# Two-head products issued in turn: 64-row tiles in the RWKV layers, 64-column tiles in the SSD layer

## The chip, the cores and the metric

The kernel runs on one core of one Trainium2 chip. TensorE (PE) multiplies; its weight loads are a row of their own in the profile (PEld). VectorE (DVE) and ScalarE (ACT) empty PSUM and do the elementwise work, GpSimd (POOL) and SyncE (SP) mostly issue transfers. The metric is the device time of one execution in microseconds, as the median of the timed runs.

## The reference

A decoder of four layers over 256 tokens of width 2048, batch 1: RWKV-7, gated linear attention (GLA), SSD (Mamba-2) and RWKV-7 again, each behind an RMS norm that is modulated by a condition vector (`ada_w`), each added back through a gate. What matters here is one step of two of the mixers.

RWKV, 32 heads of 64, written as a recurrence over tokens:

```
state = state * w_t - outer(state @ kk_t, kk_t * a_t) + outer(v_t, k_t)
y_t   = state @ r_t
```

The kernel computes it in two chunks of 128 tokens. Per head and chunk it needs products of two 64 x 128 operands over the 64 channels of a head: the 128 x 128 matrix of one operand's tokens against another's.

SSD, 64 heads of 64 in 8 groups, state 128, chunk 128:

```
y_diag = sum_j (C_i . B_j) * decay_ij * x_j      (inside a chunk)
y_off  = C_i @ state_before * exp(acum_i)        (from the chunk before)
y      = y_diag + y_off + d_skip * x
```

For each head that is two 64 x 128 results from the diagonal and one more added to the second.

## The kernel before

All activations are kept as channels on partitions, tokens along the free axis. The four layers run one after the other. A projection (`proj`, `jobs`, `prods`, line 365) streams weight blocks of 512 KB from DRAM, splits each into a high and a low fp32r part (ACT, line 310, then DVE, line 312), and multiplies three of the four cross products: three products of 128 x 128 by 128 x 256 for every 128 rows and 128 columns of weights. Meanwhile the condition's products for the next layers (`ada_group`, lines 275 to 290) are spread over the program. The code is written as a plain sequence; a list scheduler, with its own estimate of when each operand is ready, sets the order of the instructions on each engine. Tiles come from pools with a fixed number of buffers, and a tile waits until the one that had its buffer before is read out. PSUM has eight banks: two for projections (`acc`), one for the condition (`mx`), five for the stage that runs (`banks`).

An RWKV layer has a stage of its own for `rwkv_first` (run for each of eight units of two blocks, four heads, out of the evacuation of the key projection) and one for `rwkv_second` (out of the evacuation of the r projection). Both call `gram`, which is at line 750: for a head's half h (channels 0 to 63 or 64 to 127 of a block) it takes one bank from `b1` and issues four products (line 759) with 64 rows each, so that only the upper or lower half of the array's rows is used. `rwkv_first` calls it for both halves and multiplies each result by norms (line 745) on its way to `unit_inverse`; `rwkv_second` calls it three times for both halves, and a DVE multiplication by a mask empties each bank (lines 798 and 821). In the first stage `b1` has two buffers and `b2` three; in the second `b1` two, `b2` two, `b3` one. Besides `gram`, `b1` serves lines 788, 812, 814 and 882 in the second stage and 692 and 717 in the first; `b2` serves the chain 840, 845, 854 and 855 of the second stage, and the inverse in the first.

In the SSD layer, `ssd_group` runs eight times. For each of four pairs of heads it writes one bank, head u = 0 to partitions 0 to 63 and head u = 1 to 64 to 127 (half of the array's columns each): lines 1338 and 1339 the two diagonal chunks, line 1340 the part from the state, added to 1339's.

A product of plain fp32 operands shows in the trace as two MATMUL records, an fp32r product and a transpose as one.

Of the kernel before, what the change touches and what calls it, by code (L numbers as in the profile page):

```python
# [9 lines left out]
F32 = mybir.dt.float32  # L10
# [5 lines left out]
P = 128  # L16
# [115 lines left out]
class Kern:  # L132
# [55 lines left out]
    def banks(self, ctx, name, **tags):  # L188

        pool = ctx.enter_context(self.tc.tile_pool(name=name, bufs=1, space=bass.MemoryType.PSUM))  # L190

        def giver(tag, n):
            return lambda: pool.tile([P, 512], F32, name=tag, bufs=n)
        return [giver(t, n) for t, n in tags.items()]

# [303 lines left out]
    def _rwkv(self, i, j):  # L499
# [4 lines left out]
        r = self.r  # L504
# [25 lines left out]
        def mix(c):  # L530
            return [mixed(c, k) for k in range(DT)]
# [8 lines left out]
        def keeper(n, each=lambda un: None):  # L540
            def ev(jj, ps):
                t = rk.tile([P, 2, T], F32, name="sp", bufs=4)
                nc.scalar.copy(out=t, in_=ps)
                nc.gpsimd.dma_start(out=spill[n][:, jj:jj + 2, :], in_=t)
                each(jj // 2)
            return ev
# [55 lines left out]

        with ExitStack() as ctx:
            ra = ctx.enter_context(self.tc.tile_pool(name=f"ra{i}", bufs=2))
            self.b1, self.b2 = self.banks(ctx, f"pa{i}", b1=2, b2=3)
            def first(jj, ps):
                keep[jj // 2] = self.rwkv_first(i, j, jj // 2, ps, lora, ra)
            self.proj(win, D, D, mix(1), first)
        with ExitStack() as ctx:
            rb = ctx.enter_context(self.tc.tile_pool(name=f"rb{i}", bufs=2))  # L610
            self.b1, self.b2, self.b3 = self.banks(ctx, f"pb{i}", b1=2, b2=2, b3=1)

            self.St = []
            for n in range(2):
                t = rb.tile([P, 2, 2, 64], F32, name=f"St{n}", bufs=1)
                nc.gpsimd.memset(t, 0.0)
                self.St.append(t)
            units = []

            def second(un):  # L620
                units.append(self.rwkv_second(i, j, un, spill, keep[un], rb, ylast if un == 7 else None))
                next(units[un])
                if un:
                    next(units[un - 1], None)
                next(units[un])
            self.proj(win, 0, D, mix(0), keeper("r", second))
            next(units[-1], None)
# [33 lines left out]
    def rwkv_first(self, i, j, un, kps, lora, ra):  # L661
# [7 lines left out]
        NCH, C, H = 2, 128, 64  # L669
# [5 lines left out]
        def v2(t):  # L675
            return t[:, 0:512].rearrange("p (q t) -> p q t", q=2)
# [7 lines left out]
        kT, tha, S = abk[:, 0, :], abk[:, 1, :], abk[:, 2, :]  # L684
# [4 lines left out]
        for n, (nm, dst, b) in enumerate((("dec", thd, self.hw0), ("iclr", tha, self.ha0))):  # L689
            ps = self.b1()  # L690
            for q in range(2):
                nc.tensor.matmul(ps[:, q * T:(q + 1) * T], w2[0:LORA, n, q * P:(q + 1) * P], lora[nm][0:LORA],  # L692
                                 start=True, stop=True)
# [20 lines left out]
        ps = self.b1()  # L714
# [25 lines left out]
        Lf = ra.tile([P, 8 * C + 16], F32, name="LT", bufs=3)  # L740
        nc.gpsimd.memset(Lf[:, 8 * C:], 0.0)
        LT = Lf[:, 0:8 * C].rearrange("p (m t) -> p m t", t=C)
        for h in range(2):
            g = self.gram(h, [(v2(tha), v2(kT), c, q) for c in range(NCH) for q in range(2)])
            nc.vector.tensor_tensor(out=LT[:, 4 * h:4 * h + 4, :], in0=g,
                                    in1=n2[:, 4 * h:4 * h + 4].unsqueeze(2).broadcast_to([P, 4, C]), op=ALU.mult)
        Tt = self.unit_inverse(LT, Lf, ra)
# [1 line left out]
        nc.sync.dma_start(out=td, in_=Tt)  # L749
        return kd, td  # L750

    def gram(self, h, which):


        C, H = 128, 64
        ps = self.b1()
        r = slice(H * h, H * h + H)
        for n, (s, t, c, q) in enumerate(which):
            self.nc.tensor.matmul(ps[:, n * C:(n + 1) * C], s[r, q, c * C:(c + 1) * C], t[r, q, c * C:(c + 1) * C],  # L759
                                  start=True, stop=True)  # L760
        return ps.rearrange("p (n t) -> p n t", t=C)

    def rwkv_second(self, i, j, un, spill, kept, rb, last):

# [2 lines left out]
        NCH, C, H = 2, 128, 64  # L767
# [5 lines left out]
        Ac, Bc, Kc, Rc = (abkp[:, w] for w in range(4))  # L773
# [12 lines left out]
        ps = self.b1()  # L786
# [4 lines left out]
        def Gt():  # L791
            return rb.tile([P, 4, C], F32, name="G", bufs=7)

        GBR = []
        for h in range(2):
            g = self.gram(h, [(Bc, Rc, c, q) for c in range(NCH) for q in range(2)])
            GBR.append(Gt())
            nc.vector.tensor_tensor(out=GBR[h], in0=g, in1=self.c("kmask", C).unsqueeze(1).broadcast_to([P, 4, C]),
                                    op=ALU.mult)
        def prep(c):  # L800


            tk = rb.tile([P, 3, 2, P], F32, name="tk", bufs=3)
            for w0, ws in ((0, (Bc, Kc)), (2, (vT,))):
                if w0 == 0 and c == NCH - 1:
                    continue
                ps = self.b1()
                for w, src in enumerate(ws):
                    for q in range(2):
                        o, t = ps[:, (2 * w + q) * P:(2 * w + q + 1) * P], src[:, q, c * C:(c + 1) * C]  # L810
                        if w0 == 2:
                            nc.tensor.matmul(o, t, self.c("cen"), start=True, stop=True)
                        else:
                            nc.tensor.transpose(o, t, self.c("ident"))
                n = len(ws)
                nc.scalar.copy(out=tk[:, w0:w0 + n, :, :].rearrange("p w q t -> p (w q t)"), in_=ps[:, 0:n * 2 * P])
            G = []
            for h in range(2):
                g = self.gram(h, [(Kc, t, c, q) for t in (Ac, Rc) for q in range(2)])
                G.append(Gt())  # L820
                nc.vector.tensor_tensor(out=G[h].rearrange("p (w q) t -> p w q t", w=2),  # L821
                                        in0=g.rearrange("p (w q) t -> p w q t", w=2),
                                        in1=self.c("kmask").rearrange("p (w t) -> p w t", w=2).unsqueeze(2)
                                        .broadcast_to([P, 2, 2, C]), op=ALU.mult)
            return tk, G
        first = prep(0)
        yield

        yb = self.b3()
        St = self.St[un % 2]  # L830
        for c in range(NCH):
            tk, G = prep(c) if c else first
            ps = self.b2()
            for q in range(2):
                if c:
                    nc.tensor.matmul(ps[:, q * P:(q + 1) * P], Ac[:, q, c * C:(c + 1) * C], St[:, q].rearrange("p h v -> p (h v)"),
                                     start=True, stop=False)
                for h in range(2):
                    n = 2 * q + h
# [3 lines left out]
            ps = self.b2()  # L843
# [6 lines left out]
            if c < NCH - 1:  # L850
                ps = self.b2()
# [8 lines left out]
            for q in range(2):  # L860
# [3 lines left out]
                for h in range(2):  # L864
                    n = 2 * q + h
# [13 lines left out]
        ps = self.b1()  # L879
# [381 lines left out]
    def ssd_group(self, g, hs, win, acd, tk, due):  # L1261
        nc = self.nc
        sk, su = self.sk, self.su
        C, NH = 128, 64
# [18 lines left out]
        ps = self.b1()  # L1283
# [6 lines left out]
        ps = self.b1()  # L1290
# [26 lines left out]
        for c in range(2):  # L1317
            ps = self.b1()
            for v in range(4):
                nc.tensor.transpose(ps[:, v * P:(v + 1) * P], xT[:, v, c * C:(c + 1) * C], self.c("ident"))  # L1320
            t = su.tile([P, 8, 64], F32, name=f"xc{c}")
# [5 lines left out]
        ps = self.b1()  # L1327
# [4 lines left out]
        yv = su.tile([P, 4, T], F32, name="yv")  # L1332
        for v in range(4):
            ps = self.b1()
            for u in range(2):
                h = 2 * v + u
                r = slice(64 * u, 64 * u + 64)
                nc.tensor.matmul(ps[r, 0:C], xc[0][:, h, :], M[0][:, h, :], start=True, stop=True)
                nc.tensor.matmul(ps[r, C:T], xc[1][:, h, :], M[1][:, h, :], start=True, stop=False)
                nc.tensor.matmul(ps[r, C:T], st[:, h, :], ce[:, h, :], start=False, stop=True)  # L1340
            nc.vector.scalar_tensor_tensor(out=yv[:, v, :], in0=xT[:, v, :], scalar=self.p("ssd_d", 4 * g + v),
                                           in1=ps[:, 0:T], op0=ALU.mult, op1=ALU.add)
# [18 lines left out]
        ps = self.b1()  # L1361
        for c in range(2):
            nc.tensor.matmul(ps[:, c:c + 1], ss[:, c * P:(c + 1) * P], self.c("one", 0, 1), start=True, stop=True)
        r = self.inv_rms(ps, 1.0 / 512, SSM_EPS, self.b1)
# [73 lines left out]
```

## Time and profile before

| | |
|---|---|
| runs | 2950.04, 2953.18, 2945.70 us; median 2950.04 |
| profiled execution | 2968.06 us, span 2966.2 us |
| PE busy | 2840.5 us, 96% (27138 records) |
| DVE, ACT, POOL busy | 2118.3 us (71%), 1396.5 us (47%), 154.3 us (5%) |
| HBM | 226 GB/s over the span |
| mean granted TensorE clock | 0.966 |

The layers lie one after another in the span. The stage of `rwkv_first` runs at about 200 to 520 and 2300 to 2560 us, that of `rwkv_second` at 540 to 870 and 2590 to 2880, SSD from 1400 to 2100. "Busy" of a group of instructions is the time in which at least one of them was under way; since matmuls are pipelined and their records overlap, what a stretch of products costs PE is read from the starts: from the start of its first to the start of what follows it.

### The profile page before, as it was taken

How to read it: one execution, taken by the hardware profiler on the slowest of the kernel's cores; microseconds unless marked ns; L12 is line 12 of the kernel's file. 1: busy time of each engine (PE TensorE's matmuls, PEld its weight loads, DVE VectorE, ACT ScalarE, POOL GpSimd, SP SyncE). 2: the span in 40 equal slices, each digit the busy share in tenths (PEclk: the TensorE clock that was granted, in tenths of full speed). 3: DMA queues.
4: the chain of work that ended last, by engine and by line, in shares of the span. 5: the costliest groups of instructions: out<-in, count | busy, mean ns of one | idle time of the engine just before them, and what ended most of it. 6: DMA issues, size and time to landing. Idle time of an engine off the chain costs nothing.

```text
span 2966.2 us, 66151 instructions
## 1 busy us (share of the span) xinstructions
PE 2840.5 (96%) x27138; PEld 2637.4 (89%) x27138; DVE 2118.3 (71%) x4000; ACT 1396.5 (47%) x2355; POOL 154.3 (5%) x298
## 2 busy tenths in 40 slices
PE   6899999999999999998999999999889999999997
PEld 4788898899997899997999999999779989999997
DVE  5778784666777867777878786887567878565565
ACT  3475564422335544444554454544357566532233
POOL 0010110101100000000000000000001011010100
PEclk8899999999999999999999999999999999999999
DMA  9877777776666777876776666667556666675533
GB/s 341 311 266 244 238 246 248 276 242 219 215 220 209 257 268 264 290 267 213 278 253 214 218 218 219 213 200 219 172 169 222 218 197 203 204 265 159 180 119 113
DMA packets 239135, 673.82 MB, mean 227 GB/s; under 512 B 72272, under 2 KB 78416, under 8 KB 235760
## 3 DMA queue, kind: packets, MB, share of 16 engines
q1 hardware_dynamic: 217904, 580.84, 59.2%
q0 software_dynamic: 20928, 88.75, 8.4%
q8 instruction: 213, 3.49, 0.5%
q14 instruction: 90, 0.74, 0.1%
HBM read 620.66 MB, written 48.82 MB: 226 GB/s over the span
## 4 chain that ended last, share of the span: by engine, by line
PE 77%; DMA 11%; DVE 6%; issue 3%; SPq 2%; ACT 1%; POOL 0%; DVEq 0%; POOLq 0%; ACTq 0%
PE acc L365 57%; DMA raw<-in_ada_w 4%; PE b L759 3%; PE mx L275 2%; DMA raw<-in_rwkv_w_in 2%; PE pv L365 2%; DVE L L312 1%; DVE adaacc L281 1%; DMA sp<-yd 1%; PE b L868 1%; PE b L867 1%; PE b L845 1%; DMA xd<-dx 1%; PE b L692 1%; ACT H L310 1%
## 5 line engine op out<-in xcount | busy, mean ns | idle before, releaser
L365 PE MATMUL acc<-xs,H 128*128 128x256 f32 x8480 | 1635.2, 291 | 17.7 <-DVE xs L381 7.7
L365 PEld LDWEIGHTS acc<-xs,H 128*128 128x128 f32 x8480 | 1349.4, 194 | 64.1 <-issue 23.4
L365 PE MATMUL acc<-xs,L 128*128 128x256 f32 x4240 | 1225.3, 290 | 3.7 <-DVE L L312 3.7
L310 ACT CAST H<-raw 128x1024 fp32r<-128x1024 f32 (+1 forms) x706 | 718.1, 1018 | 1005.2 <-PE acc L365 745.0
L312 DVE TENSOR_TENSOR L<-raw,H 128x1024 fp32r<-128x1024 f32 (+1 forms) x706 | 835.7, 1185 | 370.7 <-ACT H L310 345.3
L365 PEld LDWEIGHTS acc<-xs,L 128*128 128x128 f32 x4240 | 822.3, 194 | 17.4 <-issue 5.8
L281 DVE SCALAR_TENSOR_TENSOR adaacc<-raw,cact,adaacc 128x512 f32<-128x512 f32 x418 | 312.5, 748 | 139.5 <-DMA raw<-in_ada_w 125.9
L365 PE MATMUL acc<-ys,H 128*128 128x256 f32 x1536 | 288.9, 287 | 2.7 <-ACT ys L380 1.9
L365 PEld LDWEIGHTS acc<-ys,H 128*128 128x128 f32 x1536 | 239.9, 191 | 14.0 <-issue 9.5
L365 PE MATMUL acc<-ys,L 128*128 128x256 f32 x768 | 219.4, 286 | 0.0
L365 PEld LDWEIGHTS acc<-ys,L 128*128 128x128 f32 x768 | 146.1, 190 | 4.5 <-issue 4.5
L275 PE MATMUL mx<-raw,cact 128*32 128x128 f32 x2416 | 118.9, 296 | 24.6 <-DMA raw<-in_ada_w 19.9
L403 DVE SCALAR_TENSOR_TENSOR x<-acc,mod,x 128x256 f32<-128x256 f32 x192 | 83.7, 478 | 54.8 <-PE acc L365 54.4
L523 ACT ACTIVATE hn<-x,mod,omu 128x256 f32<-128x256 f32 x192 | 113.2, 599 | 2.7 <-DVE x L514 1.2
L275 PEld LDWEIGHTS mx<-raw,cact 128*32 128x32 f32 x2416 | 65.9, 114 | 52.8 <-DMA raw<-in_ada_w 18.7
L759 PE MATMUL b<-abkp 64*128 64x128 f32 x768 | 105.0, 293 | 0.0
L759 PEld LDWEIGHTS b<-abkp 64*128 64x128 f32 x768 | 88.0, 193 | 13.6 <-issue 4.6
L365 PE MATMUL acc<-H,xs 128*128 128x256 f32 x512 | 97.3, 290 | 0.0
L526 DVE SCALAR_TENSOR_TENSOR xm<-x,par,hn 128x256 f32<-128x256 f32 x192 | 88.7, 479 | 1.5 <-ACT hn L523 0.3
L365 PEld LDWEIGHTS acc<-H,xs 128*128 128x128 f32 x512 | 82.4, 197 | 1.2 <-issue 1.2
L365 PE MATMUL acc<-L,xs 128*128 128x256 f32 x256 | 73.6, 289 | 0.0
L821 DVE TENSOR_TENSOR G<-b,cst 128x512 f32<-128x512 f32 x64 | 43.6, 688 | 35.7 <-PE b L759 35.1
(350 smaller groups left out, 3293.5 us busy)
## 6 DMA issues: line engine op xcount, KB each, us to landing
raw<-in_ada_w SPq DMA_DIRECT2D x384, 512.0 KB, 5.2
raw<-in_rwkv_w_in SPq DMA_DIRECT2D x256, 512.0 KB, 4.9
raw<-in_ssd_w_in SPq DMA_DIRECT2D x128, 512.0 KB, 4.7
raw<-in_gla_w_in SPq DMA_DIRECT2D x96, 512.0 KB, 4.7
raw<-in_ssd_w_out SPq DMA_DIRECT2D x64, 512.0 KB, 4.5
raw<-in_rwkv_w_out SPq DMA_DIRECT2D x48, 512.0 KB, 4.0
abkp<-kd POOLq DMA_DIRECT2D x16, 1024.0 KB, 6.9
raw<-in_gla_w_out SPq DMA_DIRECT2D x32, 512.0 KB, 5.0
```

The lines of the kernel that those rows point to most:

```text
L275: nc.tensor.matmul(ps[32 * e:32 * e + 32, 0:P], self.cact[:, k:k + 1].broadcast_to([P, 32]), raw[:, u, e * P:(e + 1) * P], start=start, st ...
L281: nc.vector.scalar_tensor_tensor(out=acc, in0=raw[:, u, :], scalar=self.cact[:, k:k + 1], in1=acc, op0=ALU.mult, op1=ALU.add)
L310: nc.scalar.copy(out=hi, in_=raw[:, a:a + n])
L312: nc.vector.tensor_tensor(out=lo, in0=raw[:, a:a + n], in1=hi, op=ALU.subtract)
L365: self.nc.tensor.matmul(ps, lhs, rhs, start=first and part == 0 and w is hi, stop=last and w is lo)
L403: nc.vector.scalar_tensor_tensor(out=self.x[:, t, 1:], in0=ps[:, u, :], scalar=gate[:, t:t + 1], in1=self.x[:, t, 1:], op0=ALU.mult, op1=A ...
L523: nc.scalar.activation(t1, x[:, k, 1:], AF.Identity, scale=self.omu[:, col:col + 1], bias=self.mods[(i, 0)][:, k:k + 1])
L526: done[k] = nc.vector.scalar_tensor_tensor(out=xm, in0=x[:, k, 0:T], scalar=self.p("rwkv_mu", col), in1=t1, op0=ALU.mult, op1=ALU.add)
L692: nc.tensor.matmul(ps[:, q * T:(q + 1) * T], w2[0:LORA, n, q * P:(q + 1) * P], lora[nm][0:LORA], start=True, stop=True)
L759: self.nc.tensor.matmul(ps[:, n * C:(n + 1) * C], s[r, q, c * C:(c + 1) * C], t[r, q, c * C:(c + 1) * C], start=True, stop=True)
L821: nc.vector.tensor_tensor(out=G[h].rearrange("p (w q) t -> p w q t", w=2), in0=g.rearrange("p (w q) t -> p w q t", w=2), in1=self.c("kmask ...
L845: nc.tensor.matmul(ps[:, n * H:(n + 1) * H], Tt[:, 4 * h + 2 * c + q, :], Rh[:, n, :], start=True, stop=True)
```

## The change

`gram` no longer takes one half h, but does both: it takes one tile `g2` of two banks and issues, for each of its four operand pairs, the product of the upper half and then that of the lower half, each half into its own bank. Its callers empty the two banks one after the other as before. The two banks come from the other pools: the first stage now has `b1` 1, `b2` 2 and `g2` one tile of two banks (before `b1` 2, `b2` 3), the second `b1` 1, `b2` 1, `b3` 1 and `g2` one tile (before 2, 2, 1). In SSD the products of the two heads of a pair are issued in turn, kind by kind.

```diff
-            self.b1, self.b2 = self.banks(ctx, f"pa{i}", b1=2, b2=3)
+            self.b1, self.b2, self.g2 = self.banks(ctx, f"pa{i}", b1=1, b2=2, g2=1)
...
-            self.b1, self.b2, self.b3 = self.banks(ctx, f"pb{i}", b1=2, b2=2, b3=1)
+            self.b1, self.b2, self.b3, self.g2 = self.banks(ctx, f"pb{i}", b1=1, b2=1, b3=1, g2=1)
...
-    def gram(self, h, which):
+    def gram(self, which):
         C, H = 128, 64
-        ps = self.b1()
-        r = slice(H * h, H * h + H)
+        both = self.g2()
+        ps = [both[:, h, :] for h in range(2)]
         for n, (s, t, c, q) in enumerate(which):
-            self.nc.tensor.matmul(ps[:, n * C:(n + 1) * C], s[r, q, c * C:(c + 1) * C], t[r, q, c * C:(c + 1) * C],
-                                  start=True, stop=True)
-        return ps.rearrange("p (n t) -> p n t", t=C)
+            for h in range(2):
+                r = slice(H * h, H * h + H)
+                self.nc.tensor.matmul(ps[h][:, n * C:(n + 1) * C], s[r, q, c * C:(c + 1) * C], t[r, q, c * C:(c + 1) * C],
+                                      start=True, stop=True)
+        return [p.rearrange("p (n t) -> p n t", t=C) for p in ps]
...
-            for u in range(2):
-                h = 2 * v + u
-                r = slice(64 * u, 64 * u + 64)
+            hr = [(2 * v + u, slice(64 * u, 64 * u + 64)) for u in range(2)]
+            for h, r in hr:
                 nc.tensor.matmul(ps[r, 0:C], xc[0][:, h, :], M[0][:, h, :], start=True, stop=True)
+            for h, r in hr:
                 nc.tensor.matmul(ps[r, C:T], xc[1][:, h, :], M[1][:, h, :], start=True, stop=False)
+            for h, r in hr:
                 nc.tensor.matmul(ps[r, C:T], st[:, h, :], ce[:, h, :], start=False, stop=True)
```

The lines of the changed kernel stand two to three lower: 365 is 367 there, 759 is 762, 788 is 791, 840 is 841, 845 is 846, 854 and 855 are 855 and 856, 867 and 868 are 868 and 869, 1338 to 1340 are 1339, 1341 and 1343. A name such as `b_6725` is a bank of `b1`, `b2` or `b3` with the number of its tile, `g_6709` one tile of two banks.

PE in the second RWKV stage, the products of one unit's second chunk, before:

```order
L759 MATMUL b_6725<-abkp 128x128 x4
L365 MATMUL acc<-xs,H 128x256
L365 MATMUL acc<-xs,L 128x256
L285 MATMUL mx<-adaacc,cst 32x128
L845 MATMUL b_6694<-Rh,Tt 128x64 x4
L854 MATMUL b_6701<-tk 64x64
L759 MATMUL b_6732<-abkp 128x128 x4
L285 MATMUL mx<-adaacc,cst 32x128 x3
```

The same unit's chunk in the changed kernel:

```order
L841 MATMUL b_6671<-tk,G 128x64 x4
L762 MATMUL g_6709<-abkp 128x128 x6
L883 MATMUL b_6660<-cst,Y 128x128 x4
L868 MATMUL b_6670<-tk,G 128x64
L762 MATMUL g_6709<-abkp 128x128 x2
L367 MATMUL acc<-xs,L 128x256
L846 MATMUL b_6678<-Rh,Tt 128x64 x4
```

The two visits of four products of one half have become one of six and one of two, and in both the halves alternate; the lone product of line 854 has left its place between them.

PE in the first RWKV stage, one unit before (`b_3451` takes the upper half, `b_3457` the lower):

```order
L275 MATMUL mx<-raw,cact 32x128 x5
L759 MATMUL b_3451<-abk 128x128
L759 MATMUL b_3457<-abk 128x128
L759 MATMUL b_3451<-abk 128x128 x3
L759 MATMUL b_3457<-abk 128x128 x3
L275 MATMUL mx<-raw,cact 32x128 x3
```

The same unit in the changed kernel:

```order
L367 MATMUL acc<-xs,L 128x256
L367 MATMUL acc<-xs,H 128x256
L762 MATMUL g_3449<-abk 128x128 x8
L367 MATMUL acc<-xs,H 128x256
L367 MATMUL acc<-xs,L 128x256
```

Before, the scheduler had put the first product of each half side by side and then three of each half in a row; now all eight alternate.

PE in the SSD layer, the products of the first group, before (up to the second of its four pairs in the later piece):

```order
L1339 MATMUL b_17239<-M_16856,xc_17214 64x128
L1338 MATMUL b_17247<-M_16845,xc_17207 64x128
L1339 MATMUL b_17247<-M_16856,xc_17214 64x128
L275 MATMUL mx<-raw,cact 32x128 x8
L1340 MATMUL b_17223<-ce,st 64x128
L1338 MATMUL b_17223<-M_16845,xc_17207 64x128
L1339 MATMUL b_17223<-M_16856,xc_17214 64x128
L1340 MATMUL b_17223<-ce,st 64x128
L1340 MATMUL b_17231<-ce,st 64x128
```

The same group in the changed kernel:

```order
L1339 MATMUL b_17207<-M_16813,xc_17175 64x128 x2
L1341 MATMUL b_17207<-M_16824,xc_17182 64x128 x2
L1339 MATMUL b_17215<-M_16813,xc_17175 64x128 x2
L1341 MATMUL b_17215<-M_16824,xc_17182 64x128 x2
L277 MATMUL mx<-raw,cact 32x128 x2
L1343 MATMUL b_17191<-ce,st 64x128 x2
L1343 MATMUL b_17199<-ce,st 64x128 x2
```

Before, the first piece held the eight diagonal products of the heads u = 0 alone, and the later piece the state's part of u = 0 and all of u = 1; now each row of two is one product of u = 0 and one of u = 1, the first piece has sixteen products and the second eight.

## Rows read from the trace of the kernel before

**Rows 1.** Windows of three stages: length, busy time and records by engine, clock, DMA.

```profile
540.00:870.00 330.00, 325.12 (x2695) 301.24 (x2692) 219.25 (x417) 98.75 (x160) 31.13 (x57) 0.96 0.68 231
1400.00:2100.00 700.00, 700.00 (x6191) 672.44 (x6190) 538.99 (x1018) 345.94 (x503) 4.85 (x9) 1.00 0.67 222
...
2590.00:2880.00 290.00, 285.57 (x2379) 268.90 (x2378) 169.45 (x334) 89.87 (x150) 31.82 (x59) 0.98 0.55 184
```

**Rows 2.** Windows of line 759 alone: length, PE and PEld busy, clock, DMA.

```profile
230.00:520.00 290.00, 15.15 (x128) 12.09 (x128) 0.97 0.74 244
...
2300.00:2560.00 260.00, 17.97 (x128) 13.55 (x128) 0.97 0.65 201
...
sum 1180.00, PE 138.15 PEld 113.60; mean PE 34.54 PEld 28.40
```

**Rows 3.** Timeline of PE, second stage: start, length, line, operands, records.

```profile
645.47 0.28 PE L365 MATMUL acc<-xs,L 128*128 128x256 f32 x1
645.59 0.28 PE L365 MATMUL acc<-xs,H 128*128 128x256 f32 x1
645.80 1.16 PE L759 MATMUL b<-abkp 64*128 64x128 f32 x8
646.88 0.39 PE L365 MATMUL acc<-xs,H 128*128 128x256 f32 x1
647.10 0.28 PE L365 MATMUL acc<-xs,L 128*128 128x256 f32 x1
...
648.68 0.33 PE L854 MATMUL b<-tk 128*64 128x64 f32 x2
```

**Rows 4.** Timeline of PE, three more visits of line 759.

```profile
285.00 1.49 PE L759 MATMUL b<-abk 64*128 64x128 f32 x16
...
410.89 0.49 PE L759 MATMUL b<-abk 64*128 64x128 f32 x4
...
656.14 0.71 PE L759 MATMUL b<-abkp 64*128 64x128 f32 x4
```

**Rows 5.** Timeline of PEld: the loads of two visits.

```profile
410.88 0.30 PEld L759 LDWEIGHTS b<-abk 64*128 64x128 f32 x4 [0.20 <-DVE abk L735]
...
645.80 0.96 PEld L759 LDWEIGHTS b<-abkp 64*128 64x128 f32 x8
```

**Rows 6.** Timeline of PE, first SSD group.

```profile
1464.20 0.43 PE L1338 MATMUL b<-M,xc 128*64 128x128 f32 x2
1464.47 0.38 PE L1339 MATMUL b<-M,xc 128*64 128x128 f32 x2
1464.68 0.38 PE L1338 MATMUL b<-M,xc 128*64 128x128 f32 x2
...
1466.09 0.64 PE L275 MATMUL mx<-raw,cact 128*32 128x128 f32 x16
1466.66 0.32 PE L1340 MATMUL b<-ce,st 128*64 128x128 f32 x1
...
1469.43 0.50 PE L365 MATMUL acc<-xs,H 128*128 128x256 f32 x2
```

**Rows 7.** Timeline of PE, lines 854 and 855 in turn.

```profile
653.33 0.27 PE L855 MATMUL b<-U,tk 128*64 128x64 f32 x1
653.34 0.27 PE L854 MATMUL b<-tk 128*64 128x64 f32 x1
...
653.94 0.43 PE L868 MATMUL b<-U,G 128*128 128x64 f32 x2
```

**Rows 8.** Groups by line: busy, mean ns of one, idle before it and its releaser.

```profile
L821 DVE TENSOR_TENSOR G<-b,cst 128x512 f32<-128x512 f32 x64 | 43.6, 688 | 35.7 <-PE b L759 35.1 <-PE b L867 0.4
L816 ACT COPY tk<-b 128x256 f32<-128x256 f32 (+1 forms) x48 | 21.3, 443 | 74.3 <-PE b L814 53.7 <-PE b L812 20.1
```

**Rows 9.** Windows of PE: length, busy, clock, DMA.

```profile
750.00:760.00 10.00, 9.82 (x65) 0.55 0.78 261
760.00:770.00 10.00, 10.00 (x72) 0.77 0.40 133
```

More of the change, by code (lines that the diff above doesn't have):

```diff
@@ L192, in giver @@
         def giver(tag, n):
+            if tag == "g2":
+                return lambda: pool.tile([P, 2, 512], F32, name=tag, bufs=n)
             return lambda: pool.tile([P, 512], F32, name=tag, bufs=n)
@@ L742, in rwkv_first @@
         LT = Lf[:, 0:8 * C].rearrange("p (m t) -> p m t", t=C)
-        for h in range(2):
-            g = self.gram(h, [(v2(tha), v2(kT), c, q) for c in range(NCH) for q in range(2)])
+        for h, g in enumerate(self.gram([(v2(tha), v2(kT), c, q) for c in range(NCH) for q in range(2)])):
             nc.vector.tensor_tensor(out=LT[:, 4 * h:4 * h + 4, :], in0=g,
@@ L794, in rwkv_second @@
         GBR = []
-        for h in range(2):
-            g = self.gram(h, [(Bc, Rc, c, q) for c in range(NCH) for q in range(2)])
+        for h, g in enumerate(self.gram([(Bc, Rc, c, q) for c in range(NCH) for q in range(2)])):
             GBR.append(Gt())
@@ L817, in prep @@
             G = []
-            for h in range(2):
-                g = self.gram(h, [(Kc, t, c, q) for t in (Ac, Rc) for q in range(2)])
+            for h, g in enumerate(self.gram([(Kc, t, c, q) for t in (Ac, Rc) for q in range(2)])):
                 G.append(Gt())
```

## The prediction

> **What bounds the kernel now.** I read the page's busy shares first (PE 96%), then windows by stage, then line 759 alone, then PE's timeline at the places that the change touches. The stages in question are PE's: PE is busy for 325.1 of 330 us and 285.6 of 290 us in the two stages of `rwkv_second` and for all 700 us in SSD, at a mean clock of 0.96 to 1.00, while the DMA engines are at 0.55 to 0.68 and DVE at 0.58 to 0.77 [rows 1]. So a product that PE finishes sooner is worth its time, unless a new wait eats it. The reader is to see that "busy" says nothing of how well the array is used: half of its rows lie idle in line 759.
>
> **What a visit of line 759 costs.** I call a run of these products without another line between them a visit. One half's four products (8 records) are busy for 1.16 us, and the next line starts 1.08 us after the first [rows 3]. Four records of one half take 0.71 us [rows 4], so a step from record to record in one half is (1.16 - 0.71) / 4 = 0.11 us. Around a visit there is more: the first record comes 0.21 us after the projection's record where two of those are 0.12 us apart, and behind the visit the second record again comes 0.22 us after the first [rows 3]: 0.09 + 0.10 us per visit, beside what lies in the 1.08.
>
> **What alternation gives.** The kernel before already has a few alternated products, by its scheduler's chance. The visit of four records at 410.89 is one product of each half: busy 0.49 us, against 0.71 us for four of one half [rows 4]. That is 0.71 less two steps, so the two halves ran side by side, and at full gain. The visit at 285.00 has 16 records, of which the order puts a pair in turn first, then three products of each half; it is busy 1.49 us, where 16 in single file would take 1.16 + 8 x 0.11 = 2.04. So even halves that merely follow each other run partly side by side before the change, and I must count real visits, not products.
> The weight loads go the same way: four alternated loads take 0.30 us, eight of one half 0.96 us, so four in single file would take 0.96 - 4 x 0.11 = 0.52 [rows 5].
> A rule of the Trainium skill speaks against this change: "TensorE: Matmul & The Clock Gate", section on LDWEIGHTS, says that a load's time goes by its columns, and that one of fewer rows takes no less. If the loads of the two halves also had to queue, 128 columns of weights for 128 of moving data would leave nothing to win; rows 5 show that they do not queue, in a visit of four.
>
> **The sum for the RWKV products.** Before, 125 visits, busy 138.15 us in all [rows 2]. In the changed order I count 109 visits: 34 of 7 or 8 products, 22 of 5 or 6, 23 of 3 or 4, 30 of 1 or 2. All alternate, so 8 products take the 8 steps of one half's four today: 1.16 us; the others are two steps (0.22 or 0.23 us) less each: 0.94, 0.71 and the measured 0.49. That is 39.4 + 20.7 + 16.3 + 14.7 = 91.1 us, or 47.0 less. Sixteen visits fewer save 0.19 us each around them, less the 0.08 by which each visit's busy time reaches into the next line: 1.7 us. Together 48.7 us: about 14 of it in `rwkv_first` (all sixteen visits fewer are there), where line 759 took 15.2 + 18.0 us [rows 2] and 22 of the visits now take 20.4, the rest in `rwkv_second`. Bounds: no overlap at all would be 109 x (1.16 - 4 x 0.223) + 512 x 0.223 = 143 us, 5 us worse than now; the upper end is the sum itself.
>
> **SSD.** Steps are 0.11 us here too: records of 1338 and 1339 start 0.21 to 0.22 us apart in twos. A group has two visits: 16 records from 1464.20 to 1466.09, 1.89 us, and 32 from 1466.66 to 1469.43, 2.77 us [rows 6]. The first will hold 16 products in 8 pairs, again 16 steps: 1.89 us. The second holds 8 products in 4 pairs: 8 steps and the same rest (1.89 - 16 x 0.109 = 0.15): 1.02 us. 1.75 us a group, eight groups: 14.0 us. That two column halves do run side by side is to be seen where 855 and 854 start 0.01 us apart and 14 records of them pass in 0.61 us [rows 7]. Without overlap the edit is worth nothing; I take 14.
>
> **Lines 854 and 855.** With one buffer of `b2`, 854's lone early product goes: each of the 16 units had it as a visit of its own (0.33 us less 0.08 of tail, and 0.19 around it [rows 3]) and 14 more records of both lines in 0.61 us [rows 7]. The sixteen records now stand together, two products of one half and then two of the other: 0.67 us if the halves overlap as now, 1.1 if not. I take 0.2 us a unit, 3 us, between 0 and 6.
>
> **Waits that come in.** Fewer banks: the first stages take a bank again 152 times, the second ones 202 times (`b1` 78, `b2` 78, `g2` 46). An evacuation is 0.69 us on DVE for a bank of products, 0.44 on ACT [rows 8]; `g2` needs two of the former, and both can stand behind a split of an L or H tile of about 1.2 or 1.0 us. So PE should have some 2 to 2.5 us of other work between the last write of a bank and the first of the next tile. I counted the instructions that stand between them in the changed order at the durations above: typically 3 to 5 us; in the second stages 24 of the 202 have under 2.5 us. What is missing adds up, over both RWKV layers, to 5 us if 2.0 us are needed, 14 at 2.5 and 35 at 3.0. Queued behind such a wait is the projection itself, since PE takes its instructions in order. At the low end all of PE's present idle time in the second stages goes: 4.9 + 4.4 = 9 us [rows 1]. I take 6 us more, from -9 to +35. Then the clock: from 750 to 770 us, in the second stage, the granted clock was 0.55 and 0.77 of full over 10 us each, though PE was busy nearly throughout [rows 9]: 13.6 us at the lower level, 1.2 instead of 2.4 GHz, at a cost of 6.8 us. One such stretch more or fewer is 7 us either way. And some of the 14 us of `rwkv_first` may sink into its chain of transfers: I take 3 of them as lost.
>
> **The sum.** -48.7 - 14.0 - 3 + 6 + 3 = -57 us. Against the profiled execution's own 2968.06 us that is 2911. The median of the runs is 18 us below that execution; I take the same saving there: 2950.04 - 57 = 2893 us.
>
> **Rivals.**
> *Only the first pair of a visit overlaps.* For it: the trace shows no long alternated run. Against it: at 285.00 more than a pair did. Then visits of 8, 6, 4 and 2 products take 1.82, 1.38, 0.93 and 0.49 us, together 128 us; 12 us instead of 49 from the RWKV products: 2930 us. Chance 0.05.
> *The loads queue,* as weighed above: RWKV's products gain nothing, SSD and 854 keep 17 us, waits take 9 and the products' own 3: 2945 us. Chance 0.02.
> *The second stages are paced by something else* once PE is faster, the transfers first of all. For it: DMA share 0.78 in 750:760 [rows 9]. Against: 0.68 over the stage, and PE's idle there is 5 us of 330 [rows 1]. What remains is SSD and `rwkv_first`, some 22 us: 2928 us. Chance 0.03.
> *Slower: the single banks.* `b1` and `b2` with one buffer each in the second stages make PE stand at each of the 202 reuses. If each costs an evacuation that nothing covers, 0.6 us, that is 121 us against the 66 saved: 3005 us. It decides from 66 / 202 = 0.33 us per reuse. For it: DVE and ACT do stand waiting for these products now and start at once when they end, 35.1 and 73.8 us in rows 8, so there is no slack on that side. Against it: the order's 3 to 5 us in between. Chance 0.04.
> The skill's "TensorEngine Tiling (Array Packing)", section "PSUM Bottleneck", says the same in general, that emptying PSUM may bind once tiling has made PE faster. No row here shows it yet: DVE is busy for 219 of 330 us in that stage [rows 1].
>
> **How the numbers follow.** The forecast holds with 0.86: 2893, its own range 2872 to 2922 (the waits' bounds, the clock and 854). With the 0.08 just above it only partly inside, I give 2872 to 2926. A measurement of this kernel tells a change from none at about 0.3%, 9 us, so below 2941 is faster: 0.86 + 0.05 + 0.03, less a little for the forecast's tail, 0.93. Within 0.3%: 0.03. Slower: 0.04.
>
> **What would show it.** Line 762 busy for about 91 us instead of 138, its visits of 16 records at 1.16 us; in SSD a group's second visit at about 1.0 us. PE's idle time in 540 to 870 and its counterpart at most 10 us over the present 9. The prediction is wrong if visits of 16 records last over 1.5 us (overlap), or if PE waits for 816, 822, 843 or 848 in many places with over 0.3 us each (banks), or if the stages keep their length while PE's busy time falls (another bound).

## The result and the profile after

The changed kernel takes 2913.37 us (median of four runs, 2904.66 to 2918.82) against 2947.87 us for the kernel before on the same chip: ratio 0.9884, 95% interval 0.9848 to 0.9920, or 34.5 us less. A second measurement gave a ratio of 0.9903 (0.9884 to 0.9922), with medians 26.4 us apart. The forecast was 57 us less, 2893 us: the sign is right, the time lies in the range, and between two fifths and a good half of the forecast gain is missing. The profiled execution takes 2918.82 us (span 2916.8), 49.2 us less than that of before, whose own execution had stood 18 us above its median; this one stands 5.5 us above.

I read the products first. The windows of line 762, the old 759 (length, PE and PEld busy with records, clock, DMA share, GB/s), answer to [rows 2]:

```profile
230.00:520.00 290.00, 10.37 (x128) 8.27 (x128) 0.95 0.75 245
540.00:870.00 330.00, 36.66 (x384) 27.94 (x384) 0.97 0.73 251
2270.00:2530.00 260.00, 11.02 (x128) 8.81 (x128) 0.92 0.62 192
2540.00:2860.00 320.00, 35.30 (x384) 27.07 (x384) 1.00 0.59 196
sum 1200.00, PE 93.36 PEld 72.09; mean PE 23.34 PEld 18.02
```

PE's busy time there went from 138.15 to 93.36 us, the loads' from 113.60 to 72.09, for the same 1024 records. PE's timeline in the second stage shows single visits (start, length, line, records) and answers to [rows 3, 4 and 7]:

```profile
563.02 1.16 PE L762 MATMUL g<-abkp 64*128 64x128 f32 x16
564.11 0.38 PE L367 MATMUL acc<-xs,H 128*128 128x256 f32 x1
...
641.45 0.34 PE L855 MATMUL b<-tk 128*64 128x64 f32 x4
...
642.11 0.43 PE L869 MATMUL b<-U,G 128*128 128x64 f32 x2
...
644.81 0.49 PE L762 MATMUL g<-abkp 64*128 64x128 f32 x4
...
679.82 0.73 PE L762 MATMUL g<-abkp 64*128 64x128 f32 x10
...
687.36 0.94 PE L762 MATMUL g<-abkp 64*128 64x128 f32 x12
```

Sixteen records now take the 1.16 us that eight of one half took, twelve take 0.94, four 0.49: both halves run at full speed side by side. The sixteen records of lines 855 and 856 pass in 0.66 us from 641.45 to 642.11. PEld, to set beside [rows 5]:

```profile
563.02 0.97 PEld L762 LDWEIGHTS g<-abkp 64*128 64x128 f32 x16
...
684.51 0.30 PEld L762 LDWEIGHTS g<-abkp 64*128 64x128 f32 x4
```

Sixteen loads of two halves take what eight of one half took, so the loads of the two row halves don't queue. The Trainium skill's "TensorEngine Tiling (Array Packing)", section "Key Properties", says that different tiles can load and multiply in parallel; this trace agrees, at 1.16 and 0.97 us. SSD's first group answers to [rows 6]:

```profile
1439.89 0.44 PE L1339 MATMUL b<-M,xc 128*64 128x128 f32 x4
...
1441.79 0.41 PE L277 MATMUL mx<-raw,cact 128*32 128x128 f32 x4
1442.13 1.09 PE L1343 MATMUL b<-ce,st 128*64 128x128 f32 x16
1443.16 0.63 PE L277 MATMUL mx<-raw,cact 128*32 128x128 f32 x12
```

The first visit lasts 1.90 us as before; the second, with all sixteen records of 1343 together, lasts 1.03 us from start to start, where sixteen of its line and sixteen of its neighbours took 2.77.

So PE's work shrank as forecast. Where is the rest? The windows by stage (length; PE, PEld, DVE, ACT, POOL busy; clock; DMA share; GB/s) answer to [rows 1]; the first and fourth are the two stages of `rwkv_first`:

```profile
200.00:520.00 320.00, 308.97 (x4135) 281.81 (x4134) 244.34 (x500) 184.63 (x355) 30.91 (x60) 0.96 0.76 251
540.00:870.00 330.00, 322.25 (x2879) 300.52 (x2878) 235.84 (x448) 106.02 (x171) 28.17 (x52) 0.97 0.73 251
1400.00:2100.00 700.00, 691.89 (x6210) 661.37 (x6209) 542.06 (x1030) 341.44 (x497) 5.19 (x9) 0.99 0.68 224
2270.00:2560.00 290.00, 276.18 (x3667) 257.96 (x3666) 205.81 (x435) 166.00 (x320) 30.10 (x58) 0.93 0.62 194
2560.00:2860.00 300.00, 297.66 (x2670) 281.31 (x2669) 192.43 (x377) 105.59 (x173) 31.82 (x59) 1.00 0.59 196
```

The second stages look as they should: 7.8 and 2.3 us without PE, DVE busy for 236 of 330 us. The fourth row does not: PE is idle for 13.8 of 290 us at a clock of 0.93. The same window of before:

```profile
2270.00:2560.00 290.00, 287.75 (x3581) 269.28 (x3580) 226.63 (x473) 180.16 (x346) 35.78 (x72) 0.97 0.66 207
```

There it was idle for 2.3 us. What PE waited for in that stretch after the change (line, released by: us in all, times, longest; the view lists waits over 0.15 us):

```profile
PE acc L367 <- DVE L L314: 4.9, 3, 3.2
PE b L719 <- ACT abk L697: 4.5, 1, 4.5
PE b L959 <- DMA Tn<-xd: 2.3, 2, 2.0
PE acc L367 <- DVE xs L383: 1.1, 1, 1.1
PE b L965 <- ACT P L961: 1.0, 1, 1.0
```

Of the second of these, PE's timeline shows both ends, and what follows:

```profile
2399.35 1.13 PE L694 MATMUL b<-lo_iclr,w 96*128 96x256 f32 x4
...
2401.85 0.73 PE L965 MATMUL b<-P,To 16*32 16x16 f32 x64 [1.01 <-ACT P L961]
2407.05 1.87 PE L719 MATMUL b<-cst,thd 128*128 128x2 f32 x8 [4.47 <-ACT abk L697]
...
2409.14 0.63 PE L367 MATMUL acc<-xs,H 128*128 128x256 f32 x2
...
2409.78 0.63 PE L367 MATMUL acc<-xs,H 128*128 128x256 f32 x2
```

Line 719 needs the only bank of `b1`, which 694 wrote from 2399.35 on; ACT empties it with line 697, of 0.4 us, but comes to it only at 2406.18 behind its other work. Then the clock (PE's windows: length, busy, clock, DMA; to set beside [rows 9]):

```profile
2390.00:2400.00 10.00, 10.00 (x157) 1.00 0.83 295
2400.00:2410.00 10.00, 4.52 (x84) 0.69 0.61 180
2410.00:2420.00 10.00, 10.00 (x106) 0.62 0.34 104
```

After the pause three projection records take 0.64 us (2409.14 to 2409.78) where they take 0.36 at the 0.12 us of [rows 3], and over 10 fully busy us the granted clock is 0.62, a mix of 2.4 and 1.2 GHz. This pause is paid for twice. (The clock can be low without such a pause: in the first window of [rows 9] PE was busy for 9.82 of 10 us.)

### The profile page after: what moved, and what is told of

It is laid out like the page before. It is cut to its first block, busy times and chain, and to the rows that moved or that the text cites. A ratio compares the mean times of both kernels' runs of the same rounds, so it can differ in the third digit from the quotient of the medians.

```text
span 2916.8 us, 66210 instructions
## 1 busy us (share of the span) xinstructions
PE 2782.8 (95%) x27138; PEld 2584.9 (89%) x27138; DVE 2116.8 (73%) x4000; ACT 1397.7 (48%) x2355; POOL 154.2 (5%) x298
## 4 chain that ended last, share of the span: by engine, by line
PE 76%; DMA 5%; DVE 5%; issue 1%; ACT 1%; SPq 1%; POOL 0%; DVEq 0%; ACTq 0%; POOLq 0%
PE acc L367 58%; PE g L762 2%; PE mx L277 2%; DMA raw<-in_ada_w 2%; DMA rv<-rd 1%; DVE L L314 1%; PE b L869 1%; PE b L846 1%; PE b L868 1%; PE b L841 1%; PE b L791 1%; DMA sp<-yd 1%; PE b L694 1%; PE b L996 1%; PE b L982 1%
## 5 line engine op out<-in xcount | busy, mean ns | idle before, releaser
L367 PE MATMUL acc<-xs,H 128*128 128x256 f32 x8480 | 1640.3, 291 | 16.7 <-ACT xs L382 6.4
L762 PE MATMUL g<-abkp 64*128 64x128 f32 x768 | 72.0, 296 | 2.8 <-DVE abkp L784 2.6
L762 PEld LDWEIGHTS g<-abkp 64*128 64x128 f32 x768 | 55.0, 189 | 17.6 <-issue 8.2
L1257 DVE SCALAR_TENSOR_TENSOR cva<-cvp,hcw,cva 128x256 f32<-128x256 f32 x144 | 64.8, 480 | 0.0
```

Of the source, the lines that this page charges most:

```text
L367: self.nc.tensor.matmul(ps, lhs, rhs, start=first and part == 0 and w is hi, stop=last and w is lo)
L762: self.nc.tensor.matmul(ps[h][:, n * C:(n + 1) * C], s[r, q, c * C:(c + 1) * C], t[r, q, c * C:(c + 1) * C], start=True, stop=True)
L1257: nc.vector.scalar_tensor_tensor(out=a, in0=src[:, k:k + T], scalar=w[k], in1=a, op0=ALU.mult, op1=ALU.add)
```

## The experiments

Times are medians, ratios against the kernel before on the same chip (2945 to 2948 us). For every profile I also worked out each RWKV stage's waits: its length in the trace, less what its products in their order would take at the steady steps of [rows 3 to 7] (0.12 us per projection record, 0.11 per step of line 759, 0.19 around a visit, and so on). What remains is pauses and half-clock time. These figures are estimates of mine and stand in no view; each comes from one profiled execution, and work and waits of the two kinds of stage together miss the profiled spans by up to 9 us. "First" sums the two stages of `rwkv_first`, "second" those of `rwkv_second`; "work" is PE's work by the same steps in the whole kernel, against before.

| kernel | gram tile in the first stages | us | ratio (95%) | work | first | second |
|---|---|---|---|---|---|---|
| before | two of `b1`, scheduler's choice | 2947 | 1 | 0 | 26.0 | 16.1 |
| ssdonly | as before | 2938.11 | 0.9968 (0.9951-0.9985) | -11.6 | 16.7 | 0.2 |
| the change | one of two banks | 2913.37 | 0.9884 (0.9848-0.9920) | -66.6 | 47.9 | 14.1 |
| after_again | one of two banks | 2921.42 | 0.9903 (0.9884-0.9922) | -66.6 | 51.3 | 10.3 |
| b1two | one of two banks | 2942.18 | 0.9973 (0.9954-0.9991) | -61.9 | 47.7 | 36.4 |
| poolsonly | one of two banks | 2962.73 | 1.0051 (1.0029-1.0074) | -19.6 | 59.0 | 16.5 |
| merged2 | one of two banks | 2906.99 | 0.9867 (0.9841-0.9892) | -68.1 | 39.3 | 16.9 |
| firsthalf | one of two banks | 2924.49 | 0.9921 (0.9903-0.9938) | -60.7 | 52.8 | 13.0 |
| firstold | single banks | 2895.35 | 0.9815 (0.9794-0.9836) | -56.1 | 19.2 | 14.7 |
| b2two | single banks | 2902.52 | 0.9854 (0.9825-0.9883) | -56.1 | 18.7 | 6.3 |
| b1one | single banks | 2900.96 | 0.9848 (0.9819-0.9878) | -50.0 | 15.7 | 16.3 |
| b1one_b2two | single banks | 2904.88 | 0.9847 (0.9823-0.9871) | -50.0 | 16.7 | 19.5 |
| firstpair | single banks, in turn | 2896.73 | 0.9838 (0.9811-0.9866) | -63.5 | 24.5 | 16.5 |
| firstpair_again | single banks, in turn | 2899.65 | 0.9842 (0.9819-0.9864) | -63.5 | 25.5 | 17.1 |

The column "first" falls into two groups without overlap: 39 to 59 us with a tile of two banks, 16 to 26 with single banks. A simpler count of the same traces, without any steps, finds the same groups: PE's idle time plus the clock that was not granted while PE was busy, from the first product of `rwkv_first` to the first of `rwkv_second`, over both layers, comes to 46 to 72 us with a tile of two banks and 22 to 36 with single banks. The profiled execution of poolsonly lies 15 us above the median of its eleven, so its 59 is on the high side. The experiments came to the two groups by way of theories that fell.

**Theory A: the single `b1` of the first stages makes PE wait at 719.** Its rivals: the short `b2` does; the alternation does; the waits are this one execution's.

*after_again*, the changed kernel once more.

> The changed kernel once more, on the chip of the three other runs. Saved 34 us at the median so far (2913 against 2948). Both theories: 2905 to 2920. In its profile, theory A (the single bank b1 in the stage of rwkv_first makes PE wait) expects again one or more pauses of PE of 1 to 5 us before lines 719, 965 or 982 in that stage, followed by stretches at the lower clock; theory B (that stage is bound by the chain of the inverse, whatever the banks) expects PE's pauses to stand mostly before 959 and 367, for transfers and for L.

Measured 2921.42 us, just above the forecast's 2920; the waits of the first stages are the same by the table, 47.9 and 51.3 us. In the second of the first stages PE again waits before 719 (3.0 us) and 987 (2.1), as theory A has it, but also before 367 for L (7.9) and before 959 for a transfer (2.2), as B has it. The pause at 719 is no accident of one execution; which theory holds, this run does not tell.

*b1two*:
```diff
-self.b1, self.b2, self.g2 = self.banks(ctx, f"pa{i}", b1=1, b2=2, g2=1)
+self.b1, self.b2, self.g2 = self.banks(ctx, f"pa{i}", b1=2, b2=1, g2=1)
```


> In the stages of rwkv_first alone, b1 gets two buffers and b2 one (the change: one and two); everything else as changed. Theory A (b1 is what PE waits for): the pause before line 719 goes, 10 to 20 us off the changed kernel, 2893 to 2903. Theory B (the chain binds): no gain, 2910 to 2920; rival within A: b2's single buffer makes the same waits at 965, 982, 987, and the time is 2915 to 2930.

Measured 2942.18 us, outside what either theory gave. A second `b1` bought with a `b2` is worse than the change by 21 us: the first stages wait as long as before it, and 22 to 26 us more of waits stand in the second stages. Theory A's gain did not come. The edit did more than it was meant to: in the trace the first layer's last product of the inverse starts at 590 us, at 530 in the change, and the first of `rwkv_second` at 615 instead of 550, so the run is no clean test of `b1`.

*firstold*, the first stages as before, the rest as changed:
```diff
-self.b1, self.b2, self.g2 = self.banks(ctx, f"pa{i}", b1=1, b2=2, g2=1)
+self.b1, self.b2 = self.banks(ctx, f"pa{i}", b1=2, b2=3)
...
-for h, g in enumerate(self.gram([...])):
+for h in range(2):
+    g = self.gram1(h, [...])          # one bank of b1, four products, as before
```


> The stages of rwkv_first as before the change (b1 two, b2 three, half after half); rwkv_second and SSD as changed. Theory A and B both say that the first stages lose nothing then: PE's saved time is 34 + 14 + 3 us from the rest, so 2948 - 51 + 6 = 2903, 10 us faster than the whole change, if what the change saves in the first stages (14 us by the sum) is more than lost there to waits. If the first stages do gain under the change and the shortfall lies in the second ones, this kernel is slower than the changed one: 2920 to 2928.

Measured 2895.35 us, 52 to 55 less than before and 26 less than the whole change on the same chip. So second stages and SSD alone bring more than the whole change, and the edit of the first stages costs 26 us where the forecast had it save 11.

*poolsonly*, the change's pools, but every product half after half and SSD as before:
```diff
-for n, (s, t, c, q) in enumerate(which):
-    for h in range(2):
+for h in range(2):
+    for n, (s, t, c, q) in enumerate(which):
```


> The pools of the change without its order: gram takes the tile of two banks but issues four products of one half, then four of the other; SSD as before. Counted from its order, 35 of 99 visits hold both halves in a row, which the trace of before shows at 1.71 us against 2 x 1.16: PE saves some 20 us. Theory A: the single bank's waits (20 to 25 us) eat that, 2940 to 2955. Theory B: 2925 to 2935.

Measured 2962.73 us, above what either theory gave and slower than before although its PE work is 20 us less. The waits are there without any alternation, so the pools bring them.

**Which of the pools?** The second set took the version with the old first stages and made one pool short at a time.

*b2two*: `b1=2, b2=2` in place of `b1=2, b2=3`.

> The first stages as before the change (half after half, b1 two) but with two buffers of b2 in place of three, one bank left idle; rwkv_second and SSD as changed. The order of every engine is the same as with three, so only a wait at run time can differ. Theory A (b1 is what the first stage lacks): as with three, 2890 to 2900. Rival (the inverse lacks the third b2): 2905 to 2920.

Measured 2902.52 us (0.9854), between the two ranges, with 18.7 us of waits; instructions stand in the same order as in firstold on every engine, and the time is the same within the intervals. The third `b2` bank was not needed.

*b1one*:
```diff
-self.b1, self.b2 = self.banks(ctx, f"pa{i}", b1=2, b2=3)
+self.b1, self.b2, self.gb = self.banks(ctx, f"pa{i}", b1=1, b2=3, gb=1)
...
-    ps = self.b1()                    # in gram1
+    ps = self.gb()
```


> The first stages half after half with b2 three, one bank for lines 692 and 717 and one bank of its own for gram, so that each has a single buffer; rwkv_second and SSD as changed. Theory A (a single bank for 692 and 717): PE's own work is 6 us more than with the old first stage, and the waits of the change come back, 10 to 20 us: 2910 to 2922. Rival (b2, or the tile of two banks, does it): 2897 to 2905.

Measured 2900.96 us and 15.7 us of waits: with a single `b1` for 692 and 717, and one single bank for the gram products, nothing is lost. Theory A falls for good.

*merged2*, the change with the two products of line 692 written into halves of a `g2` tile, `b1` for 717 alone:
```diff
+both = self.g2()
...
-ps = self.b1()
+ps = both[:, n, :]
```


> The change, but in the first stages the two products of line 692 take the two halves of one g2 tile, and b1's single bank is left to line 717 alone. PE's own work by the rows' durations is 12 us less than with the old first stage. Theory A (717 stood behind 692's evacuation in one bank): the waits go and the gain of the first stages comes through, 2880 to 2893. Rival B (the chain of the inverse binds PE there, whatever it saves): 2895 to 2905. If the tile of two banks makes the next waits: 2905 to 2920.

Measured 2906.99 us, ratio 0.9867 against after_again's 0.9903, some 11 us better with intervals that overlap a little; waits 39.3. That is the time forecast for the case that the tile of two banks makes the next waits. Relief for `b1` helps at most a little and leaves most of the waits.

*firstpair*, old pools in the first stages, the products in turn into two `b1` tiles:
```diff
+ps = [self.b1() for h in range(2)]    # in the first stages, in place of the two halves of a g2 tile
```


> The first stages with the pools of before (b1 two, b2 three), gram issued in turn into two tiles of b1; the scheduler keeps part of the alternation (36 visits). PE's own work is 7 us less than with the old first stage. Theory A: 2886 to 2895, faster than the old first stage, since no bank is taken away. Rival B (chain): as the old first stage, 2893 to 2900.

Measured 2896.73 us: PE's work is 7 us less than in firstold, its waits 5 us more, and the time cannot be told from firstold's. It lies in rival B's range and just above theory A's: that the chain of the inverse takes what PE saves there is not ruled out for a saving this small.

**Theory T: the tile of two banks, taken and handed back as one.** Its rival C: the short pools `b1 = 1` and `b2 = 2` together. Two kernels whose source differs in the gram tile alone tell them apart.

*b1one_b2two*: b1one with `b1=1, b2=2, gb=1`.

> First stages with one buffer of b1, two of b2 (as many as the change has) and a single bank of their own for the gram products, half after half; the rest as the change. Theory T (what brings the waits is that the products of both halves must find two banks free at once and hand them back together): waits of the first stages about 16 us in all, 2897 to 2907 us, like the version with three buffers of b2 (2901). Rival C (the change's short pools b1 = 1 with b2 = 2 together, whichever tile the gram has): waits of 40 us or more as in the change, 2915 to 2930 us.

*firsthalf*: the change, but in the first stages alone the two halves of its two-bank tile are written one after the other.
```diff
+turns = [(n, h) for n in range(len(which)) for h in range(2)]
+if apart:                             # true for the call in rwkv_first
+    turns.sort(key=lambda x: x[1])
```


> The changed kernel with its pools and its two-bank tile everywhere, but in the first stages the products are written half after half; it differs from the kernel above in nothing but the gram tile of the first stages. Theory T: the waits of the first stages stay (40 to 60 us in all) although nothing alternates there, 2915 to 2935 us. Rival C: the same as the kernel above, within 5 us. If alternation itself brought the waits, they would go: about 2900 us.

Measured on one chip: 2904.88 and 2924.49 us, ratios 0.9847 (0.9823 to 0.9871) and 0.9921 (0.9903 to 0.9938). Both have `b1` 1 and `b2` 2 and write half after half; the two-bank tile costs 20 us more. First-stage waits are 16.7 and 52.8 us, second-stage waits 19.5 and 13.0, work is 10.7 us less in firsthalf: 36.1 - 6.5 - 10.7 = +18.9, against 19.6 between the medians and 17.8 between the profiled spans. Rival C falls, and so does alternation as a cause. The reason that theory T gave is not shown with it. PE itself hardly waits for the tile: its idle times of over 0.15 us before the first stages' gram products come to 1.0 us in firsthalf and 1.4 in b1one_b2two, and there is none in the change (3.5 in merged2, where line 692 takes such tiles too). The extra pauses stand elsewhere, before the inverse's products (12.3 us in firsthalf, 6.2 in b1one_b2two), the projection's (7.2 and 4.8) and those of lines 694 and 719 (5.5 and none). And the scheduler makes another order of the two kernels: the last gram product of the first of these stages starts at 430 us in firsthalf and at 460 in b1one_b2two. PE's longest waits in 2270 to 2560, of firsthalf (its lines from 760 on stand three below the change's):

```profile
PE acc L367 <- DVE L L314: 4.6, 2, 3.8
PE b L719 <- ACT abk L697: 2.3, 1, 2.3
PE acc L367 <- ACT H L312: 1.8, 1, 1.8
```

and of b1one_b2two (its lines from 760 on stand about ten below), all that there are:

```profile
PE b L969 <- DMA Tn<-xd: 2.2, 1, 2.2
PE acc L367 <- DVE L L314: 1.7, 1, 1.7
PE gb L759 <- DVE LT L747: 1.4, 1, 1.4
```

The clocks of the same window (columns as in the windows by stage) go along. Of firsthalf:

```profile
2270.00:2560.00 290.00, 278.57 (x3621) 260.43 (x3619) 206.91 (x440) 165.57 (x319) 29.35 (x57) 0.94 0.62 194
```

and, of b1one_b2two:

```profile
2270.00:2560.00 290.00, 284.78 (x3755) 265.04 (x3754) 213.53 (x451) 172.64 (x334) 29.99 (x58) 0.98 0.64 203
```

The longest pause of firsthalf's first stages shows what such a wait can be made of. PE:

```profile
404.93 0.69 PE L985 MATMUL b<-Tn,LT 32*32 32x32 f32 x16
...
412.44 0.90 PE L985 MATMUL b<-Tn,LT 32*32 32x32 f32 x13 [4.04 <-ACT P L986]
```

ACT in the same stretch:

```profile
405.37 1.65 ACT L978 COPY Tt<-T 32x256 f32<-32x256 f32 x4
410.95 1.04 ACT L312 CAST H<-raw 128x1024 fp32r<-128x1024 f32 x1 [3.93 <-DMA raw<-in_rwkv_w_in]
412.02 0.36 ACT L986 COPY P<-b 32x256 f32<-32x256 f32 x1
```

PE waits 4.04 us for a copy of 0.36 us, which stands in ACT's queue behind the split of a weight block that has not landed: ACT had waited 3.93 us for it. The projection, which could fill the time, stands behind 985 in PE's queue. Its weights were there: DVE had made the L parts of its next two blocks by 395.92 and 398.18 us,

```profile
394.72 1.20 DVE L314 TENSOR_TENSOR L<-raw,H 128x1024 fp32r<-128x1024 f32 x1
...
396.97 1.21 DVE L314 TENSOR_TENSOR L<-raw,H 128x1024 fp32r<-128x1024 f32 x1
```

and at 24 products to a block, 7 of the first and all of the second were still to do when the pause began: 31 products, 3.7 us at 0.12 us each. The link that fails differs from version to version (719, 985, 367, 959).

*ssdonly*, the SSD edit alone.

> Only the SSD edit, everything in RWKV as in the kernel before. SSD's products should give 14 us as the profile of the change shows for that stage: 2931 to 2935 us against 2946. If what SSD gains is given back behind it (the next stage waits for transfers): within 5 us of before.

Measured 2938.11 us, 0.9968 (0.9951 to 0.9985), 4 to 14 us less: the forecast's 14 is just inside the interval, and the time is 3 us above the range given for it. In the trace the old line 1340's busy time of 19.57 us became 8.75 in SSD's 700 us, the same as in the whole change (8.76).

*firstpair_again*.

> The version with the first stages' pools of before and their products written in turn into two b1 tiles, once more beside the others: 2893 to 2902 us if it was read rightly, ratio 0.982 to 0.985.

Measured 2899.65 us, 0.9842: with firstold among the fastest versions, 12 to 19 us better than the change by the ratios.

## Why the prediction was right, and where it fell short

**The overlap of the row halves: right in mechanism and size.** Line 762 is busy for 93.4 us (forecast 91.1), its visits of 16 records take 1.16 us as forecast. The rivals of a single overlapping pair and of queued loads are out. What the second stages gain can be read from two runs: firstold adds their edit to ssdonly, which has only SSD's, and stands 45 us lower by the ratios; b2two, which differs from firstold only in an idle bank, 34. The forecast's terms give 34 + 3 - 6 = 31, so this part came out at least as well as forecast.

**SSD and lines 855 and 856: right.** A group's second visit lasts 1.03 us (forecast 1.02); 855 and 856 pass in 0.66 us (forecast 0.67). From the first product of `ssd_group` to its last, SSD takes 685.1 and 685.6 us in the two traces without the edit (before, poolsonly) and 671.2 to 673.3 in the twelve with it, 12 to 14 us less; ssdonly's timing allows it, though its middle is 9.

**The single banks of the second stages: rival rightly given little.** Waits there are 14.1 and 10.3 us in the change, 16.1 in the profile of before and 0.2 in that of ssdonly, whose RWKV instructions stand as before. Against the mean of the latter two the change adds 2 to 6 us, so the +6 was fair. G's multiplications still take 0.68 us and the copies of `tk` 0.44, as in [rows 8]:

```profile
L822 DVE TENSOR_TENSOR G<-g,cst 128x512 f32<-128x512 f32 x64 | 41.4, 684 | 9.5 <-PE g L762 8.2 <-PE b L868 1.0
L818 ACT COPY tk<-b 128x256 f32<-128x256 f32 (+1 forms) x48 | 21.2, 443 | 77.6 <-PE b L814 49.7 <-PE b L816 27.9
```

The Trainium skill's "TensorEngine Tiling (Array Packing)", section "PSUM Bottleneck", warned that emptying PSUM may bind: here the emptying engines' throughput does not (DVE 236 of 330 us). What binds in the two pauses shown above is an evacuation's turn in ACT's queue.

**The term that was mis-sized** is the last line of "Waits that come in": "some of the 14 us of `rwkv_first` may sink into its chain of transfers: I take 3 of them as lost". The term came out at 37 us more: by firstold the edit of the first stages costs 26 us instead of saving 11. All 14 sank, and more: the change's first stages wait 47.9 and 51.3 us, against 26.0 in the profile of before and 16.7 in that of ssdonly. I had counted bank reuses and their cover for the second stages alone, where the pools looked shortest, and for the first only the number of reuses (152). Nor are the last releasers mostly transfers: of PE's 25.3 us of idle time there in the change, ACT ends 8.8 us, DVE 7.9 and a transfer 3.4. The bounds of the waits, -9 to +35, were drawn for the wrong stages, and it is luck that they were wide enough. It is luck too that the rest of the change gained 52 to 55 us where its terms gave 46: 37 us on top of 2893 alone would have been 2930, outside the range.

**The move from the profile to the median was the other half.** Of the 20 us between 2893 and 2913, 8 stand between the two profiled executions (2919 measured, 2911 by the sum). The other 12.5 are the 18 us by which the execution of before stood above its median, of which the changed one kept 5.5. That execution had 42 us of RWKV waits (26.0 + 16.1), the profile of ssdonly, with the same order in RWKV but 10.5 us below the median of its own runs, 17: part of what I subtracted on top was a scatter of waits, and the change's 62 us, alike in its two profiles, took its place. If the waits of before are put at the mean of the two, 30 us, which two executions can only suggest, the sum comes to -66.6 of work + 32 of waits = -35, measured -34.5 and -26.4.

One rival's figure was added up wrongly: SSD and `rwkv_first` alone come to 14 + 14 - 3 = 25 us by the prediction's own terms, not "some 22"; nothing else rests on it.

**What stays open.** That the two-bank tile of the first stages brings the waits is shown by the pair of kernels whose source differs in nothing else. How it does so is only argued: a unit's evacuations and its step into the inverse may come in a bunch, and the scheduler's order may put them before projection work that was ready, as in the pause at 412. A wait for the two banks themselves it is not, as PE's idle time before the gram products shows; whether the order alone would do it, with the banks free, no run tells, since each edit also makes another order. Of the 7 us of work that firstpair saves, its own waits take 5 by the table; why they rise is open too.

## What to carry to other kernels

Issue small products in turn on the two halves of the array wherever PE bounds the stage: the gain can be read beforehand from a few visits that happen to alternate. Price the PSUM tile that makes it possible in every stage where it comes in: it was not the number of banks that cost time here (b1one_b2two has pools as short as the change's), but the tile of two. In this kernel the old pools were better in the stage with few such products (22 of 109 visits) and long chains through ACT, DVE and transfers. Before adding the distance of one profiled execution to the median onto a forecast, find out what that distance consists of; if it is waits, the change has waits of its own.

## What the runs showed of the hardware that was not expected

A pause of PE of 4 to 5 us costs more than its length: around the one from 2402 to 2407 the granted clock was 0.69 and 0.62 over two windows of 10 us, though PE was fully busy in the second; around firsthalf's, which ends at 412, it was 0.66 from 410 to 420. SSD's 128 loads of line 1340 (1343 after) were busy for 11.97 us before and 6.82 after (length, PE and PEld busy, clock, DMA):

```profile
1400.00:2100.00 700.00, 19.57 (x128) 11.97 (x128) 1.00 0.67 222
...
1380.00:2080.00 700.00, 8.76 (x128) 6.82 (x128) 1.00 0.69 228
```

The loads keep step with the products; whether the loads of two column halves run side by side, as those of two row halves do, these times do not tell.
